# A planner's costs, homes and priorities changed in a two-layer hybrid decoder trunk

## The chip, the core and the metric

The kernel runs on one core of one Trainium2 chip. Times are device microseconds (us) of that core from the start to the end of one execution; the median of three is compared. A profile is one further execution taken by the hardware profiler. In it PE is TensorE (matrix products), PEld its loading of weights, DVE is VectorE, ACT is ScalarE, POOL is GpSimd and SP is the engine whose queue issues the DMA transfers. The text also uses the code's letters for them: V for DVE, A for ACT, G for POOL, Q for the DMA queue.

## The reference

16 meta tokens are put before 512 tokens of width 1024, and two layers run over the 528 rows, all in float32. Each layer is a half-step gated feed-forward network (FFN), a mixing block and a second FFN, with a norm before and after each:

```python
h = h + 0.5 * rms_norm(swiglu(rms_norm(h, g[0]), ffn_w_in[l, 0], ffn_w_out[l, 0]), g[1])
z = rms_norm(h, g[2]) @ w_in[l]            # 1024 -> 2476 columns
fq, fk, fv, ff, cu, lx, lg, dq, dkv, iq, ik, iw = jnp.split(z, split_at, axis=-1)
y_fox  = forgetting_attention(...)         # 4 heads x 64, keys q, k, v and a forget gate
y_conv = conformer_conv(cu, ...)           # gate, 31 taps per channel, layer norm, silu
y_lru  = rg_lru_branch(lx, lg, ...)        # 4 taps, a linear recurrence, times gelu(lg)
y_dsa  = dsa_attention(dq, dkv, iq, ik, iw, ...)   # 8 index heads choose 128 keys per query
mix = concatenate([y_fox, y_conv, y_lru, y_dsa]) @ w_out[l]
h = h + rms_norm(mix, g[3])
h = h + 0.5 * rms_norm(swiglu(rms_norm(h, g[4]), ffn_w_in[l, 1], ffn_w_out[l, 1]), g[5])
```

The index scores of a query are relu(q_idx . k_idx) summed over 8 heads with weights; the 128 best keys of each query are then attended to. The output is h without the meta rows.

## The kernel before

Activations lie with channels on the partitions and the 528 tokens along the free axis, in two halves of 264. Every weight is split on the chip into two fp32r parts, a copy by ACT (`wh`, `whi`) and the remainder by DVE or POOL (`wl`, `wlo`); a product x.W is three matmuls (hi.hi, hi.lo, lo.hi), 264 columns each. A weight tile of `w_in` or of the FFN is 1024 wide and split in two pieces of 512 in most places; an early tile of `w_out` is six rows of 128, split in two pieces of 384.

The mixing block of a layer (`mix`) goes through these steps. Four leading products (two for index queries, two for the recurrence), five token blocks (`token_block`: forget gate, latent, index key, index weight), then the column units (`column`) in the order of the string `ORDER`: c is the convolution's gate and value, v the attention's values, f its queries and keys, g the recurrence's gelu, q the queries of the sparse attention. Beside them run the index scores (`scores`: one matmul `psa<-KS,QS` per head and block, a relu by ACT into `rl`, and a multiply-add by DVE into `msel`), the choice of 128 keys (`choice`: 16 rounds of MAX8 and MATCH_REPLACE8 on DVE for each of four blocks), the 31 taps of the convolution (`conv_taps`: 8 taps per channel block on DVE as `cv<-hp,taps,cv`; the other 21 as a product by ACT into the one buffer `cm` and an add by POOL, `cv<-cv,cm`), the recurrence, and two attentions. Then comes the output projection: `early` adds up six of the eight row blocks, `late_rows` the last two, the sparse attention's; SP loads 15 early tiles and 2 late ones in each layer.

What runs when is not left to the hardware: a planner, `Weave`, builds the program. Every part above is a stream, a Python thread which stops before each instruction. `pick` takes the stream whose next instruction can start first by simulated clocks of PE, A, V, G and Q; among those that want the same engine and could start no more than `AHEAD` later, the one with the lowest `RANK` wins. `cost` gives the length of an instruction, `LATENCY` the time from one engine to another, `pace` multiplies PE's cost by 1.82 while TensorE's clock is taken to be halved, and `port` holds the intervals in which DVE and POOL exclude one another. The order that comes out is fixed on PE, A, V and G by dependencies between neighbours on an engine, so the chip executes each of these engines' work in just that order, and an instruction that is not ready holds up all behind it. All instructions of the planner are issued in `issue`, so that every one has line L252 in the profile; they are told apart by the names of their tiles.

Small elementwise operations have a home in the table `ENG`: V, G, or E for "whichever of the two ends first by the clocks". `wlead`, `wcol`, `wearly` and `wlate` are the weights' splits in the mixing block, `gelu` and `gate` scalings on either side of an activation function (tiles `xg` and `cv`), `rconv`, `rlru` and `rdsa` the splits of a branch's result into `ycat`. `SUMS` is the home of the adds of squares `acc`. PSUM has eight banks: two `u`, five `a`, one `n`; letter x in `LB` (leading FFN products) and `TB` (tails) takes `u` and `a` in turn.

## Time and profile before

| | us |
|---|---|
| median of 3 runs | 2126.69 (2126.13 to 2129.04) |
| profiled execution | 2126.25 |
| its span, first to last instruction | 2124.5 |
| PE busy in it | 2005.0 (94%) |
| DVE, ACT, POOL busy | 1252.5, 899.4, 475.3 |
| mean granted TensorE clock | 0.973 of full |

The span is 1.75 us shorter than the execution's time. In time order the span holds: the start (0 to 40 us), the first FFN of layer 0 (to 340), its mixing block (340 to 765), the second FFN (to 1055), a seam between the layers (to 1112), the first FFN of layer 1 (to 1425), its mixing block (to 1805), its second FFN (to 2095) and the end. In the page's picture of 40 slices PE shows a 9 through the FFNs and 7 or 8 in the mixing blocks, DVE 8 and 9 there and 3 or 4 elsewhere; the clock shows an 8 in the slices of the mixing blocks and a 9 in the rest.

### The profile page before, as it was taken

The numbers are of one execution on the slowest core, as the hardware profiler recorded it, in microseconds if no ns is written. First come the engines' busy times: TensorE is split into PE (matmuls) and PEld (weight loads), VectorE is DVE, ScalarE is ACT, GpSimd is POOL, SyncE is SP. The second block draws the span as 40 slices with busy tenths as digits, with TensorE's granted clock in tenths as the row PEclk, the third lists the DMA queues.
The fourth block names the chain that finished last, engine by engine and source line by source line (L and its number), as shares of the span: only waits on it lengthen the run. The fifth ranks groups of instructions, "written<-read, shape, count | busy, mean of one in ns | idle before, by whom it ended". The sixth has DMA issues, their size and how long they took to land.

```text
span 2124.5 us, 37005 instructions
## 1 busy us (share of the span) xinstructions
PE 2005.0 (94%) x14579; PEld 1880.8 (89%) x14579; DVE 1252.5 (59%) x2881; ACT 899.4 (42%) x1891; POOL 475.3 (22%) x429
## 2 busy tenths in 40 slices
PE   7999999978999899999989999999879998999998
PEld 7999999877878899999979999998768788888886
DVE  5434435889985843444384344447899958434444
ACT  5332233456765533222343322324568655332232
POOL 2101012336631110101221010123356412111121
PEclk9999999988999999999999999999889999999999
DMA  4432323211113233233223323322111132332321
GB/s 136 119 101 81 100 60 95 54 40 41 38 45 94 70 97 103 80 100 90 70 60 100 100 80 103 97 66 64 40 40 38 46 100 70 119 109 89 100 98 42
DMA packets 311078, 168.71 MB, mean 79 GB/s; under 512 B 15968, under 2 KB 302952, under 8 KB 310904
## 3 DMA queue, kind: packets, MB, share of 16 engines
q1 hardware_dynamic: 310616, 165.97, 26.9%
q8 instruction: 114, 1.87, 0.4%
q14 instruction: 60, 0.49, 0.1%
q10 hardware_dynamic: 288, 0.39, 0.1%
HBM read 164.22 MB, written 2.10 MB: 78 GB/s over the span
## 4 chain that ended last, share of the span: by engine, by line
PE 55%; DVE 21%; ACT 2%; issue 2%; SPq 1%; DMA 1%; POOL 0%; DVEq 0%; ACTq 0%; POOLq 0%
PE psa L252 39%; PE psu L252 15%; DVE msel L252 4%; DVE m L252 2%; DVE cv L252 2%; DVE hn L252 2%; PE psn L252 2%; DVE lra L252 2%; DVE acc L252 1%; DVE h L252 1%; DVE lrb L252 1%; SPq L252 1%; DVE x L252 1%; DMA wraw<-in_w_out_dram 1%; DVE rows L252 1%
## 5 line engine op out<-in xcount | busy, mean ns | idle before, releaser
L252 POOL TENSOR_TENSOR ga<-ga 128x264 f32<-128x264 f32 (+1 forms) x160 | 139.6, 874 | 1058.0 <-DVE ga L252 974.2
L252 ACT ACTIVATE whi<-wraw 128x512 fp32r<-128x512 f32 (+4 forms) x260 | 193.8, 757 | 248.7 <-PE psa L252 128.9
L252 PE MATMUL psa<-x,wh 128*128 128x264 f32 (+2 forms) x1228 | 244.8, 294 | 12.1 <-DVE x L252 4.7
L252 DVE TENSOR_TENSOR wlo<-wraw,whi 128x1024 fp32r<-128x1024 f32 (+4 forms) x179 | 179.4, 1008 | 122.1 <-ACT whi L252 120.1
L252 PE MATMUL psu<-x,whi 128*128 128x264 f32 (+1 forms) x1176 | 240.7, 300 | 6.1 <-DVE fq L252 2.7
L252 ACT ACTIVATE wh<-wraw 128x1024 fp32r<-128x1024 f32 (+3 forms) x188 | 151.3, 817 | 216.7 <-PE psa L252 117.1
L252 DVE TENSOR_TENSOR ga<-psa,R 128x264 f32<-128x264 f32 (+1 forms) x244 | 102.2, 428 | 233.5 <-PE psa L252 225.8
L252 DVE TENSOR_TENSOR wl<-wraw,wh 128x1024 fp32r<-128x1024 f32 (+3 forms) x161 | 161.4, 1011 | 127.4 <-ACT wh L252 126.3
L252 PE MATMUL psa<-x,whi 128*128 128x264 f32 (+2 forms) x1188 | 231.3, 291 | 1.0 <-DVE ga L252 1.0
L252 PEld LDWEIGHTS psa<-x,wh 128*128 128x128 f32 x1228 | 194.5, 189 | 20.4 <-DVE x L252 8.0
L252 PEld LDWEIGHTS psu<-x,whi 128*128 128x128 f32 x1176 | 192.8, 196 | 10.7 <-issue 4.2
L252 PEld LDWEIGHTS psa<-x,whi 128*128 128x128 f32 x1188 | 189.0, 191 | 2.9 <-DVE ga L252 1.1
L252 PE MATMUL psa<-x,wl 128*128 128x264 f32 (+2 forms) x614 | 178.4, 290 | 0.8 <-POOL wl L252 0.8
L252 PE MATMUL psa<-x,wlo 128*128 128x264 f32 (+2 forms) x594 | 173.1, 291 | 4.8 <-DVE wlo L252 4.8
L252 PE MATMUL psu<-x,wlo 128*128 128x264 f32 (+1 forms) x588 | 174.7, 298 | 0.0
L252 POOL TENSOR_TENSOR wlo<-wraw,whi 128x512 fp32r<-128x512 f32 (+1 forms) x81 | 116.2, 1440 | 235.9 <-ACT whi L252 207.1
L252 ACT ACTIVATE G<-ga 128x264 fp32r<-128x264 f32 (+1 forms) x160 | 67.5, 422 | 231.8 <-POOL ga L252 230.3
L252 PE MATMUL psa<-G,whi 128*128 128x264 f32 x852 | 156.4, 284 | 0.0
L252 PE MATMUL psa<-ycat,wh 128*128 128x264 f32 (+2 forms) x660 | 150.1, 318 | 3.8 <-DVE ycat L252 3.3
L252 POOL TENSOR_TENSOR cv<-cv,cm 128x528 f32<-128x528 f32 x84 | 126.4, 1505 | 91.7 <-ACT cm L252 91.6
L252 PEld LDWEIGHTS psa<-G,whi 128*128 128x128 f32 x852 | 131.8, 188 | 0.0
L252 DVE TENSOR_TENSOR G<-ga,G 128x264 fp32r<-128x264 f32 (+1 forms) x160 | 77.4, 484 | 90.3 <-ACT G L252 90.1
(306 smaller groups left out, 5030.9 us busy)
## 6 DMA issues: line engine op xcount, KB each, us to landing
wraw<-in_ffn_w_in_dram SPq DMA_DIRECT2D x160, 512.0 KB
wraw<-in_ffn_w_out_dram SPq DMA_DIRECT2D x44, 512.0 KB
wraw<-in_ffn_w_out_dram SPq DMA_DIRECT2D x48, 384.0 KB
wraw<-in_w_in_dram SPq DMA_DIRECT2D x36, 512.0 KB
wraw<-in_w_out_dram SPq DMA_DIRECT2D x180, 64.0 KB
xin<-in_x_dram SPq DMA_DIRECT2D x8, 256.0 KB
wraw<-in_w_out_dram SPq DMA_DIRECT2D x8, 256.0 KB
wraw<-in_w_in_dram SPq DMA_DIRECT2D x4, 256.0 KB
```

What stands on the lines that cost most here:

```text
L252: done = call(*args, **kw)
```

## The change

No product, sum or transfer is added or taken away: PE and ACT have as many instructions as before, and DVE and POOL together as well (DVE 2755 before, 2705 after; POOL 434 and 484). The numbers by which the planner reckons change, the homes of some operations, and with both the order on every engine. In the diff the tables of priorities are cut to a line of each side; all their other entries change as well in that manner (the rank of `prep` from 19.1 to 150.7, `scores` 52.9 to 13.7, `index` 212.2 to 217.3, `row` 179.1 to 100.5, `turn1` 25 to 168.8, `conv` 0 in both).

```diff
-    AHEAD = dict(PE=0.0, A=0.05, V=0.0, G=0.3)
+    AHEAD = dict(PE=0.0, A=0.19, V=0.0, G=0.3)
...
-            self.slow = part < (0.4 if self.slow else 0.25)
+            self.slow = part < 0.385
...
-    def ported(self, key, op, aps, reads):
...
+    def hold(self, key, op, aps, args, reads):
+        banks = any(a.space == bass.MemoryType.PSUM for a in aps)
+        if key == "G" or key == "V" and not banks and op not in ("max", "match_replace"):
+            return self.cost(key, op, aps, args, reads, 0.0)
+        return 0.0
...
         if key == "PE":
+            wide, rows = args[1].free_size(), args[1].shape[0]
+            load = 0.0127 + 0.00077 * wide
+            n = args[2].free_size()
+            stream = lambda t: max(t, load) if rows > 64 else t + load * (0.9 if rows != 32 else 0.3)
             if op == "transpose":
-                n = args[1].shape[0]
-                return self.pace(start, 0.091, n * n / 128 / 2400)
-            cols, rows = args[2].free_size(), args[2].shape[0]
-            if cols == 1:
-                return 0.156
+                return self.pace(start, stream(n / 1200 + 0.002), n * rows / 128 / 1200)
             if args[2].dtype == F32R:
-                return self.pace(start, max(cols / 2400 + 0.0115, 0.092), cols * rows / 128 / 2400)
-            return self.pace(start, max(cols * 4 / 2400 + 0.005, 0.184), cols * rows / 128 / 1200)
+                return self.pace(start, stream(n / 2400 + 0.0115), n * rows / 128 / 2400)
+            return self.pace(start, 2 * stream(n / 1200 + 0.002), n * rows / 128 / 600)
         if key == "V":
             one = op in ("tensor_scalar", "tensor_copy", "memset") and not psum
-            return (n / (2 if one else 1) + 66) / 960 + 0.06 * small
+            return (n / (2 if one else 1) + 66) / 960 + 0.06 * small + 0.06 * (op == "match_replace")
         if key == "A":
-            return n / 1200 + (0.05 if psum else 0.094) + 0.094 * small
+            extra = n > 8 and sum(a.free_size() == 1 for a in aps) > small
+            return n / 1200 + (0.05 if psum else 0.094) + 0.094 * small + 0.09 * extra
...
-    LB = 'a'
-    TB = 'ax'
+    LB = 'x'
+    TB = 'ux'
...
-    ORDER = 'ccvffgqqg'
+    ORDER = 'ccvffqgqg'
...
-    SUMS = dict(tail='G', late='V', enter='E')
+    SUMS = dict(tail='V', late='V', enter='E')
...
-    ENG = dict(hadd='V', wlead='G', wt='V', wcol='G', wearly='E', wlate='G', wtail='V', wnext='E', gelu='E',
-               geluo='V', gate='V', ct='V', tapsum='E', rfox='E', rconv='E', rlru='V', rdsa='E', lrua='V',
+    ENG = dict(hadd='V', wlead='E', wt='V', wcol='G', wearly='G', wlate='V', wtail='V', wnext='E', gelu='G',
+               geluo='V', gate='G', ct='V', tapsum='E', rfox='E', rconv='V', rlru='E', rdsa='G', lrua='V',
...
-    RANK = dict(ev=0, late=48.5, weights=18.0, row=179.1, lead=42.0, index=212.2, prep=19.1, scores=52.9,
+    RANK = dict(ev=6.3, late=48.5, weights=10.8, row=100.5, lead=49.3, index=217.3, prep=150.7, scores=13.7,
```

`free` and `start_of` take the duration of `hold` where they took a yes or no of `ported`, and follow the same rule with it; the constant 424 is written `QS0[-1]`, which is 424; the scratch tiles of one reciprocal root at the end of the kernel get one name instead of four.

Over the two layers the homes move as follows. The gate's scalings (8 TENSOR_SCALAR and 8 TENSOR_TENSOR on `cv`) and the gelu's (16 and 16 on `xg`) go from DVE to POOL. Of the 60 splits of 384 columns of `w_out`, POOL does 60 where it did 6; of the splits of 512 columns it does 82 where it did 102, DVE 94 where it did 74. DVE does 134 adds of squares `acc` where it did 98, POOL 6 where it did 42. Four splits of the attention's result go from POOL to DVE, and seven others come to POOL.

On PE, in the mixing block of layer 0, the index scores before stand in one run at their end. `KS,QS` is a score matmul, its last number the keys it covers; `x,wlo` and `x,whi` are column units.

```order
L252 MATMUL psu<-x,whi 128x264 x2
L252 MATMUL psu<-x,wlo 128x264
L252 MATMUL psa<-KS,QS 106x212 x3
L252 MATMUL psa<-KS,QS 104x264 x2
L252 MATMUL psa<-KS,QS 106x318 x4
L252 MATMUL psa<-KS,QS 106x424
L252 MATMUL psa<-KS,QS 104x264 x2
L252 MATMUL psa<-KS,QS 106x424
L252 MATMUL psa<-KS,QS 104x264 x2
L252 MATMUL psa<-KS,QS 106x424
L252 MATMUL psa<-KS,QS 104x264 x2
L252 MATMUL psu<-whi,x 106x256 x2
```

After, the same block's scores begin 89 matmuls sooner, counted from the start of the first FFN's tail (83 in layer 1), and stand one by one among column units:

```order
L252 MATMUL psa<-KS,QS 106x212
L252 MATMUL psu<-x,wlo 128x264
L252 MATMUL psu<-x,whi 128x264 x2
L252 MATMUL psa<-KS,QS 106x318
L252 MATMUL psu<-x,wlo 128x264
L252 MATMUL psu<-x,whi 128x264 x2
L252 MATMUL psu<-x,wlo 128x264
L252 MATMUL psa<-KS,QS 106x424
L252 MATMUL psu<-x,whi 128x264
L252 MATMUL psa<-KS,QS 106x212
L252 MATMUL psu<-x,whi 128x264
L252 MATMUL psu<-x,wlo 128x264
```

Columns that stood ahead of the first score stand between the scores now; the last 14 scores, `106x424` and `104x264`, still stand without a column between them.

On DVE the multiply-adds of the same scores (`msel<-rl,wh,msel`) alternate before with the DVE taps of the convolution:

```order
L252 SCALAR_TENSOR_TENSOR msel<-rl,wh,msel 106x212
L252 SCALAR_TENSOR_TENSOR cv<-hp,taps,cv 128x528
L252 SCALAR_TENSOR_TENSOR msel<-rl,wh,msel 106x212
L252 SCALAR_TENSOR_TENSOR cv<-hp,taps,cv 128x528
L252 SCALAR_TENSOR_TENSOR msel<-rl,wh,msel 106x212
L252 SCALAR_TENSOR_TENSOR cv<-hp,taps,cv 128x528
L252 SCALAR_TENSOR_TENSOR msel<-rl,wh,msel 106x212
L252 SCALAR_TENSOR_TENSOR cv<-hp,taps,cv 128x528
L252 SCALAR_TENSOR_TENSOR msel<-rl,wh,msel 106x318
L252 SCALAR_TENSOR_TENSOR cv<-hp,taps,cv 128x528
```

After, they stand nearly alone, and the convolution's input `hp` and its taps come behind them:

```order
L252 SCALAR_TENSOR_TENSOR msel<-rl,wh,msel 104x528
L252 TENSOR_SCALAR lrb<-lrb 128x264
L252 SCALAR_TENSOR_TENSOR msel<-rl,wh,msel 104x528
L252 TENSOR_TENSOR lrb<-lrb 128x264
L252 SCALAR_TENSOR_TENSOR msel<-rl,wh,msel 104x528
L252 TENSOR_TENSOR lrb<-lrb 128x264
L252 SCALAR_TENSOR_TENSOR msel<-rl,wh,msel 104x528
L252 TENSOR_TENSOR hp<-cv,psu 128x264
L252 MAX m_5336<-msel 106x8
L252 MAX m_5351<-msel 106x8
L252 TENSOR_TENSOR hp<-cv,psu 128x264
L252 MATCH_REPLACE msel<-m_5336,msel 106x212
```

The first `hp` of layer 0 stood four rows ahead of the first score's add before, and stands behind all but one of the scores' adds now; in layer 1 the first taps are moved behind most of them in the same way.

On POOL at the start of layer 0's taps (`cv<-cv,cm`) before there are only weight splits between the taps:

```order
L252 MEMSET hp 128x30
L252 MEMSET lf 128x640
L252 MEMSET hp 128x30
L252 TENSOR_TENSOR wlo<-wraw,whi 128x512 x3
L252 TENSOR_TENSOR cv<-cv,cm 128x528
L252 TENSOR_TENSOR wlo<-wraw,whi 128x512
L252 TENSOR_TENSOR cv<-cv,cm 128x528
L252 TENSOR_TENSOR wlo<-wraw,whi 128x512
L252 TENSOR_TENSOR cv<-cv,cm 128x528
L252 TENSOR_TENSOR wlo<-wraw,whi 128x512
L252 TENSOR_TENSOR cv<-cv,cm 128x528
```

After, the gate's scalings of `cv` come ahead of the first tap and between the first ones (8 in each layer); among the last taps and behind them, ahead of the first split of `w_out`, stand 14 operations on `xg`.

```order
L252 MEMSET lf 128x640
L252 MEMSET hp 128x30 x2
L252 TENSOR_SCALAR cv<-cv 128x264
L252 TENSOR_TENSOR cv<-cv,R 128x264
L252 TENSOR_TENSOR wlo<-wraw,whi 128x512
L252 TENSOR_SCALAR cv<-cv 128x264
L252 TENSOR_TENSOR cv<-cv,R 128x264
L252 TENSOR_TENSOR wlo<-wraw,whi 128x512 x3
L252 TENSOR_TENSOR cv<-cv,cm 128x528
L252 TENSOR_SCALAR cv<-cv 128x264
L252 TENSOR_TENSOR cv<-cv,R 128x264
L252 TENSOR_TENSOR cv<-cv,cm 128x528
```

At the seam of the layers on PE, the products that stand between a half's sum of squares (`ones,acc`) and the spreading of its result over the partitions (`cst,rows`) are 14 before:

```order
L252 MATMUL psn<-ones,acc 88x1 x3
L252 MATMUL psa<-x,wh 128x264
L252 MATMUL psa<-x,wl 128x264
L252 MATMUL psa<-x,wh 128x264 x2
L252 MATMUL psa<-x,wl 128x264
L252 MATMUL psa<-x,wh 128x264 x2
L252 MATMUL psa<-x,wl 128x264
L252 MATMUL psa<-x,wh 128x264 x2
L252 MATMUL psa<-x,wl 128x264
L252 MATMUL psa<-x,wh 128x264 x2
L252 MATMUL psa<-x,wl 128x264
L252 MATMUL psn<-cst,rows 128x88 x3
```

After, there are 37 matmuls between the same two, products of further weight tiles (`whi`, `wlo`) among them; the first of the 37:

```order
L252 MATMUL psn<-ones,acc 88x1 x3
L252 MATMUL psu<-x,wl 128x264
L252 MATMUL psa<-x,wh 128x264 x2
L252 MATMUL psa<-x,wl 128x264
L252 MATMUL psa<-x,wh 128x264 x2
```

23 matmuls more stand in this place, and 174 instead of 130 x.W products stand in all ahead of the fourth `ones,acc`.

## Rows read from the trace of the kernel before

**Rows 1.** Stretches: length; busy (count) of PE, PEld, DVE, ACT, POOL; clock, DMA, GB/s.
```profile
40.00:340.00 300.00, 300.00 (x2464) 299.81 (x2464) 127.05 (x218) 96.16 (x161) 30.02 (x40) 1.00 0.31 91
...
455.00:610.00 155.00, 134.25 (x949) 118.14 (x948) 151.38 (x417) 103.76 (x249) 91.28 (x65) 0.92 0.13 36
...
1055.00:1112.00 57.00, 46.17 (x354) 44.99 (x353) 46.60 (x122) 25.40 (x61) 17.43 (x14) 0.94 0.20 56
...
1525.00:1675.00 150.00, 132.84 (x951) 116.47 (x949) 148.05 (x413) 105.47 (x251) 94.60 (x64) 0.94 0.14 38
```

**Rows 2.** PE's waits, 455 to 610 us: total, times, longest.
```profile
PE psa L252 <- ACT rl L252: 11.5, 9, 4.5
```

**Rows 3.** PE's waits, 1525 to 1675 us.
```profile
PE psa L252 <- ACT rl L252: 10.1, 11, 2.3
```

**Rows 4.** PE's timeline, layer 0's run of scores: start, us, instruction, idle before.
```profile
471.88 0.70 PE L252 MATMUL psa<-KS,QS 128*106 128x212 f32 x5
477.11 0.60 PE L252 MATMUL psa<-KS,QS 128*106 128x318 f32 x1 [4.53 <-ACT rl L252]
...
490.77 0.63 PE L252 MATMUL psu<-whi,x 128*106 128x256 f32 x2
```

**Rows 5.** A stretch of ten microseconds inside that run.
```profile
480.00:490.00 10.00, 4.71 (x9) 2.35 (x10) 10.00 (x15) 5.06 (x13) 4.01 (x2) 0.50 0.20 52
```

**Rows 6.** DVE's groups by line, 455 to 610 us: busy, mean ns, idle before.
```profile
L252 DVE MATCH_REPLACE8 msel<-m,msel 106x212 f32<-106x212 f32 (+3 forms) x64 | 33.4, 525 | 0.0
L252 DVE MAX8 m<-msel 106x8 f32<-106x212 f32 (+3 forms) x64 | 32.4, 532 | 0.1
```

**Rows 7.** DVE's groups by form, whole span.
```profile
L252 DVE TENSOR_TENSOR wlo<-wraw,whi 128x384 fp32r<-128x384 f32 x26 | 15.3, 597 | 10.3 <-ACT whi L252 9.5 <-DMA wraw<-in_w_out_dram 0.5
...
L252 DVE TENSOR_TENSOR xg<-xg 128x264 f32<-128x264 f32 x16 | 9.3, 593 | 0.0
L252 DVE TENSOR_SCALAR xg<-xg 128x264 f32<-128x264 f32 x16 | 7.4, 474 | 0.0
L252 DVE TENSOR_TENSOR cv<-cv,R 128x264 f32<-128x264 f32 x8 | 6.4, 805 | 0.1
L252 DVE TENSOR_SCALAR cv<-cv 128x264 f32<-128x264 f32 x8 | 5.3, 668 | 2.0 <-ACT cv L252 2.0
```

**Rows 8.** POOL's groups by form, whole span.
```profile
L252 POOL TENSOR_TENSOR ga<-ga 128x264 f32<-128x264 f32 x120 | 93.7, 781 | 818.7 <-DVE ga L252 748.3 <-ACT ga L252 28.9 <-ACT whi L252 15.3
...
L252 POOL TENSOR_TENSOR wlo<-wraw,whi 128x384 fp32r<-128x384 f32 x6 | 6.9, 1152 | 59.8 <-ACT whi L252 59.8
L252 POOL TENSOR_TENSOR ycat<-fq,ycat 128x528 fp32r<-128x528 f32 x4 | 5.6, 1416 | 0.0
...
L252 POOL MEMSET small<- 128x512 f32 x2 | 1.1, 527 | 0.0
```

**Rows 9.** DVE's timeline at two places of layer 0's gate and taps.
```profile
452.46 1.40 DVE L252 TENSOR_TENSOR cv<-cv,R 128x264 f32<-128x264 f32 x1
...
473.34 0.42 DVE L252 TENSOR_TENSOR cv<-cv,R 128x264 f32<-128x264 f32 x1
```

**Rows 10.** POOL's timeline: two splits, first and last of layer 0's 42 taps.
```profile
450.97 2.60 POOL L252 TENSOR_TENSOR wlo<-wraw,whi 128x512 fp32r<-128x512 f32 x2 [12.12 <-ACT whi L252]
...
462.69 1.61 POOL L252 TENSOR_TENSOR cv<-cv,cm 128x528 f32<-128x528 f32 x1 [1.11 <-ACT cm L252]
...
605.96 1.32 POOL L252 TENSOR_TENSOR cv<-cv,cm 128x528 f32<-128x528 f32 x1 [0.85 <-ACT cm L252]
607.43 1.00 POOL L252 TENSOR_TENSOR wlo<-wraw,whi 128x384 fp32r<-128x384 f32 x1 [0.15 <-ACT whi L252]
```

**Rows 11.** The DMA queue's waits, 590 to 720 us.
```profile
SPq L252 <- POOL wlo L252: 38.6, 3, 24.5
```

**Rows 12.** PE's timeline at the seam of the layers.
```profile
1091.60 0.90 PE L252 MATMUL psn<-cst,rows 88*128 88x88 f32 x6 [3.15 <-DVE rows L252]
...
1103.39 0.45 PE L252 MATMUL psa<-x,wlo 128*128 128x264 f32 x1 [4.65 <-DVE wlo L252]
```

## What the changed kernel was predicted to take, and why

> **What bounds the kernel now.** I read the table of stretches first [rows 1]. From 40 to 340 us, the first FFN, PE is busy 300.00 of 300.00 us at clock 1.00 with 2464 matmuls: 300 / 2464 = 0.122 us for a product of 264 columns. A planner can gain nothing there, and the other FFNs read alike. What it can gain lies in the mixing blocks. From 455 to 610 PE idles 155 - 134.25 = 20.75 us, and runs at a mean clock of 0.92, which takes another 0.08 x 155 = 12.4 us of full speed. From 1525 to 1675 it is 17.2 idle and 0.06 x 150 = 9.0 and at the seam (1055 to 1112) 10.8 and 0.06 x 57 = 3.4. In the two middle stretches DVE is busy 151.38 of 155 and 148.05 of 150 us: there PE waits, and DVE sets the pace.
>
> The waits of PE say for what it stops: 11.5 us for `rl`, the relu of the index scores, in layer 0 [rows 2], 10.1 in layer 1 [rows 3]. The releaser named is ACT, but `rl` has three buffers, and DVE's adds free them. The timeline shows the place: from 471.88 to 490.77 PE has nothing but score matmuls in its order, and stops 4.53 us after the fifth [rows 4]. In ten microseconds of it DVE is busy 10.00, PE 4.71, and the granted clock is 0.50, the lower level of 1.2 GHz [rows 5]. POOL's 42 taps run from 462.69 to 605.96 + 1.32 = 607.28, and only then comes POOL's first split of `w_out` [rows 10]; behind that SP waits 38.6 us in three pieces [rows 11].
>
> **Scores among columns, taps behind scores (both layers).** In the new order two to four columns stand between most scores, and DVE no longer alternates score adds with taps. PE is thus filled where it stopped; but the columns are only moved: 89 matmuls stand behind the first score instead of ahead of it, 89 x 0.122 = 10.9 us in layer 0, 83 x 0.122 = 10.1 in layer 1. So no more than about 11 us a layer can be filled, and the 14 last scores still stand bare. The end of the stage is DVE's: its choice of keys, 33.4 + 32.4 us in layer 0 [rows 6], has to be done before the last attentions. So the gain is what DVE has less to do before that.
>
> DVE gives away, from the totals over two layers [rows 7]: gate 5.3 + 6.4, gelu 7.4 + 9.3, together 28.4, or 14.2 a layer. It takes over two result splits a layer; POOL needed 1.42 for one [rows 8], and I put DVE at half of that, 1.4 for both: net 12.8. POOL takes the work on. Its product of 264 columns takes 0.78 [rows 8]; its TENSOR_SCALAR is in no row, and I bound it by the MEMSET of 512 columns, 0.53, and the product, 0.78, and take the nearer in kind, the MEMSET. 12 of each: 12 x 0.78 + 12 x 0.53 = 15.7 us more on POOL a layer (18.7 by the other bound).
>
> POOL's work is not free for DVE. The same gate product took DVE 1.40 us at 452.46, while POOL worked on two splits until 453.57, and 0.42 at 473.34 with POOL idle [rows 9, 10]. The rule for it, in the Trainium skill's page "SBUF — State Buffer", section "SBUF: two separate sides", is that DVE and GpSimd share a port pair as an exclusive lock, held for a whole instruction, so that the later one blocks; 1.40 against 0.42 agrees with it. By that rule alone, with every POOL operation blocking DVE, the offload would be worth nothing; that is a rival below.
>
> MAX8 and MATCH_REPLACE8 show no such stretching: their means are 532 and 525 ns with 91.28 us of POOL beside them [rows 1, 6]. They and the readers of PSUM are more than half of DVE's time here, so I let less than half of POOL's 15.7 us come back as blocking, 7: net 12.8 - 7 = about 6 a layer. Ends: -14.2 (no blocking) and +2.9 (all of it blocking, 15.7 - 12.8).
>
> Against it stands the convolution. In layer 0 the first `hp` waited four rows ahead of the first score's add and now stands behind nearly all of them; even with the scores starting some 6 us sooner, the first taps come 10 to 20 us later. Before, 42 taps took 607.28 - 462.69 = 144.6 us, 3.44 each, where the last add takes 1.32 and waited 0.85 for its `cm` [rows 10], 2.2 in all, so that they can go closer together: at 2.6, my choice nearer to 2.2, they take 109, and 22 gate and gelu operations of 14.4 us come into the same queue ahead of the first split of `w_out`. 109 + 14 + 15 is about 138, near 144.6: I take half of the 6 back in layer 0, where the taps move furthest. Layer 0: -3. Layer 1, where DVE's order to the last choice is shortened most: -6. Ends of both: -14 and +12 each.
>
> **Splits of `w_out`.** 54 splits of 384 columns leave DVE, 27 a layer, and POOL needs 1.15 for 0.60 [rows 7, 8]. Two pieces a tile make a load's split 2.3 us instead of 1.2. That hides as long as loads arrive further apart; SP's waits of this stretch are for just these splits [rows 11]. If they stood bare it would be 27 x 0.55 = 15 a layer; hidden, zero. I take +1 a layer, near the hidden end, because the first tiles queue behind POOL's taps either way.
>
> **The seam.** PE stops 3.15 us for `rows` at 1091.60, and 4.65 for `wlo` at 1103.39 [rows 12]. With `LB` on seven banks, 23 more matmuls stand ahead of the first stop, 23 x 0.122 = 2.8 us, which nearly covers 3.15. In all 44 more products stand ahead of the fourth sum, 5.4 us, so up to 8.2 if both count. `wlo` is a weight split and comes as late as before: what PE does earlier is missing there. I take -4; ends -8 and +2 (the bare wait grown).
>
> **The rest.** The adds of squares moved to DVE lie beside PE-bound FFN tails, where DVE is busy 127 of 300 us [rows 1]: nothing; were that cover gone, 36 adds at the 0.59 of DVE's product of 264 columns [rows 7] would be 21 us over the whole kernel. The renamed scratch tiles and the constant: nothing.
>
> Sum: -3 - 6 + 2 - 4 = -11, from the profiled 2126.25 to 2115. That execution lies 0.44 us below the median of 2126.69, well inside what counts here.
>
> **Rivals.**
> 1. *POOL sets the end (slower).* The taps start 15 us later, and POOL's 22 added operations (14.4 us) are not taken in by closer taps, so that the convolution's last tap comes 10 us later in layer 0 and 6 in layer 1. The early output products need the convolution's result, so PE waits for it. For it: the first split after the taps began 0.15 us after them [rows 10], the queue is full at its end. Against: POOL idles 64 us of 155 in that stretch [rows 1]. It decides once the taps' mean stays above (144.6 - 15 - 14.4) / 42 = 2.74 us. Time: 2126.25 + 10 + 6 + 2 - 4 = 2140.
> 2. *Given back.* The scores fill PE and nothing ends sooner, since the output projection waits for its loads, which queue behind the taps (38.6 us [rows 11]). Only the seam is left: 2126.25 - 4 + 2 = 2124.
> 3. *All of POOL's work blocks DVE.* +2.9 in each layer instead of -12.8: 2126.25 + 6 - 4 + 2 = 2130. This is the Trainium skill's lock, taken at its full price. Against it stand the unstretched MAX8 rows.
> 4. *The clock stays up.* With columns among the scores PE is no longer granted 0.50 in them, and half of the idle and of the missing clock of both middle stretches comes back: (20.75 + 12.4) / 2 = 16.6 and (17.2 + 9.0) / 2 = 13.1, with the seam -4 and +2 for the splits: 2094. Against: DVE's choice of keys stays where it is.
>
> **How the numbers follow.** Forecast 0.42; rivals 1: 0.18, 2: 0.20, 3: 0.07, 4: 0.13. A measurement of this kernel can tell about 0.2%, 4.3 us, from no change. The forecast's own range is 2104 to 2124, so nearly all of its chance is on the faster side (0.38), rival 4 adds 0.13, and of rival 2, which lies 2.7 us below, a quarter falls beyond the bound (0.05): faster 0.56. Rival 1 is slower nearly always, rival 3 half the time, and a little of the forecast: 0.24. Within 0.2%: 0.20. The range leaves out half of rival 4 below and about half of rival 1 above: 2095 to 2138.
>
> **What would show it.** Right: PE's wait for `rl` falls from 11.5 and 10.1 to under 5 in sum, and the stretch of scores is no longer granted 0.50; `cv<-cv,R` is no DVE row any more; the last MATCH_REPLACE8 comes some 6 us sooner than the start of its layer's scores alone explains; at the seam the 3.15 is gone. Wrong: the last tap of layer 0 comes later against the start of its stage than 607.28 - 455 = 152 us and PE waits for `cv` behind it (rival 1); or PE is filled in the scores and idles as long before the output projection (rival 2).

## The result and the profile after

The changed kernel takes 2100.57 us (median; 2100.15 to 2101.61) against 2127.86 before (2126.13 to 2132.26): ratio 0.9869 (0.9852 to 0.9886). That is 26 to 27 us faster where 11 were forecast; the direction held, the size did not. Its span is 2098.4 us, 26.1 less. Ratios, here and below, are of fast runs alone; one run of four of `after_old_ranks`, 2212.66 us, was slow and is left out of its ratio.

The table of stretches of the kernel before, cut anew at events (first sum of the FFN's tail, first index score, last POOL tap, fourth sum at the block's end), for layer 0 and then layer 1:

```profile
core 0: us, PE busy (x) PEld busy (x) DVE busy (x) ACT busy (x) POOL busy (x), PEclk, DMA share, GB/s
360.40:455.90 95.50, 85.49 (x649) 79.91 (x650) 79.05 (x230) 48.18 (x112) 30.24 (x26) 0.91 0.20 50
455.90:607.30 151.40, 131.40 (x929) 115.81 (x928) 147.81 (x411) 101.15 (x244) 89.95 (x63) 0.92 0.13 35
607.30:738.20 130.90, 116.70 (x828) 105.91 (x827) 94.76 (x260) 77.06 (x199) 21.55 (x17) 0.95 0.28 82
1428.20:1525.90 97.70, 86.42 (x650) 80.77 (x649) 78.78 (x230) 48.49 (x112) 29.97 (x26) 0.91 0.18 46
1525.90:1672.60 146.70, 130.76 (x939) 115.00 (x940) 144.81 (x407) 102.30 (x244) 92.78 (x62) 0.94 0.14 38
1672.60:1795.90 123.30, 109.06 (x808) 100.58 (x807) 94.56 (x261) 76.09 (x197) 25.13 (x21) 0.97 0.29 85
```

The same stretches of the changed kernel:

```profile
358.60:446.00 87.40, 73.27 (x564) 68.35 (x564) 74.02 (x234) 46.08 (x108) 11.46 (x12) 0.85 0.20 51
446.00:597.20 151.20, 139.54 (x993) 126.65 (x994) 143.40 (x402) 102.97 (x245) 100.97 (x81) 0.93 0.14 38
597.20:723.70 126.50, 114.51 (x850) 108.08 (x849) 81.86 (x224) 78.12 (x198) 50.65 (x53) 0.96 0.29 85
1405.20:1490.90 85.70, 71.90 (x567) 67.17 (x565) 73.86 (x234) 46.10 (x108) 11.48 (x12) 0.86 0.20 52
1490.90:1643.00 152.10, 135.19 (x996) 121.83 (x997) 148.71 (x409) 103.31 (x248) 98.53 (x80) 0.97 0.13 37
1643.00:1770.60 127.60, 111.42 (x828) 105.03 (x827) 82.28 (x218) 76.88 (x196) 53.05 (x53) 0.96 0.28 82
```

Call the three A, B and C. A is 8.1 us shorter in layer 0 and 12.0 in layer 1, with 85 and 83 fewer matmuls. B takes up 64 and 57 more and changes by -0.2 and +5.4; C by -4.4 and +4.3. The blocks give 12.7 and 2.3 us. The rest lies between them: up to the first tail's sum -1.8, second FFN of layer 0 -3.7 (319.2 to 315.5 us, where before its first 21.8 us were granted 0.84 and did 157 matmuls, now 1.00 and 182), seam with the next FFN -4.8 (370.8 to 366.0), the end -0.8. Together 26.1. A stretch of one profile scatters by some us: in `before_lead_banks` below, with the blocks' order unchanged, layer 0's C is 127.6 instead of 130.9 and its block 375.6 instead of 377.8.

PE's side of it: a block holds as many matmuls as before (2406 and 2407 records in layer 0, 2397 and 2391 in layer 1). Its busy time falls by 6.3 and 7.7 us; its idle time falls by 6.4 in layer 0 and grows by 5.4 in layer 1.

What PE waits for, in B of layer 0, of layer 1, and at the seam (1039 to 1093 us); these answer to [rows 2], [rows 3] and [rows 12]:

```profile
PE psu L252 <- DVE gt L252: 4.7, 1, 4.7
PE psa L252 <- ACT rl L252: 2.2, 4, 1.2
...
PE psu L252 <- DVE gt L252: 6.3, 2, 5.8
...
PE psa L252 <- ACT rl L252: 0.8, 1, 0.8
...
PE psn L252 <- DVE acc L252: 2.8, 1, 2.8
PE psn L252 <- DVE rows L252: 1.6, 1, 1.6
```

The wait for `rl` is all but gone, 11.5 and 10.1 down to 2.2 and 0.8; the wait for `gt`, the evacuation of a column, has grown from 1.2 and 1.4 to 4.7 and 6.3. At the seam the 4.7 for `wlo` is gone and the longest wait for `rows` is 1.6 where it was 3.2, but 2.8 for `acc` has come. POOL's taps of layer 0, first and last, and what follows [rows 10]:

```profile
475.72 1.32 POOL L252 TENSOR_TENSOR cv<-cv,cm 128x528 f32<-128x528 f32 x1
...
595.85 1.32 POOL L252 TENSOR_TENSOR cv<-cv,cm 128x528 f32<-128x528 f32 x1 [0.89 <-ACT cm L252]
599.89 0.41 POOL L252 TENSOR_SCALAR xg<-xg 128x264 f32<-128x264 f32 x1 [2.71 <-ACT xg L252]
...
607.37 1.00 POOL L252 TENSOR_TENSOR wlo<-wraw,whi 128x384 fp32r<-128x384 f32 x1
```

They start 13 us later and end 10 us sooner: 121.5 us for 42, 2.89 each, with half of the gate's and of the gelu's operations in between. Against the first score the last tap ends as before (B, 151.2 and 151.4 us), and the first split of `w_out` starts at the same time of the span, 607.37 and 607.43.

The last round of DVE's choice of keys, in layer 0 before and after, then in layer 1 before and after:

```profile
606.22 0.69 DVE L252 MATCH_REPLACE8 msel<-m,msel 104x528 f32<-104x528 f32 x1
...
582.15 0.70 DVE L252 MATCH_REPLACE8 msel<-m,msel 104x528 f32<-104x528 f32 x1
...
1694.35 0.69 DVE L252 MATCH_REPLACE8 msel<-m,msel 104x528 f32<-104x528 f32 x1
...
1631.39 0.69 DVE L252 MATCH_REPLACE8 msel<-m,msel 104x528 f32<-104x528 f32 x1
```

The choice ends 14.2 us sooner after the first score in layer 0 (151.0 to 136.8) and 28.0 sooner in layer 1 (169.1 to 141.2). From its end to the block's fourth sum it is 140.9 us where it was 131.3, and 138.5 where it was 100.9.

The forms that are new on POOL, over the whole span [rows 7, 8]:

```profile
L252 POOL TENSOR_TENSOR wl<-wraw,wh 128x384 fp32r<-128x384 f32 x32 | 32.7, 1040 | 46.2 <-ACT wh L252 33.3 <-DMA wraw<-in_w_out_dram 12.4 <-PE psa L252 0.4
...
L252 POOL TENSOR_TENSOR xg<-xg 128x264 f32<-128x264 f32 x16 | 13.8, 861 | 0.8
L252 POOL TENSOR_SCALAR xg<-xg 128x264 f32<-128x264 f32 x16 | 9.2, 572 | 14.4 <-DVE rows L252 8.1 <-ACT xg L252 5.8
...
L252 POOL TENSOR_TENSOR cv<-cv,R 128x264 f32<-128x264 f32 x8 | 7.4, 930 | 0.7
L252 POOL TENSOR_SCALAR cv<-cv 128x264 f32<-128x264 f32 x8 | 4.9, 614 | 51.3 <-ACT cv L252 51.3
```

### The profile page after: what moved, and what is told of

It is laid out like the page before. It is cut to its first block, busy times and chain, and to the rows that moved or that the text cites. A ratio compares the mean times of both kernels' runs of the same rounds, so it can differ in the third digit from the quotient of the medians.

```text
span 2098.4 us, 36992 instructions
## 1 busy us (share of the span) xinstructions
PE 1989.9 (95%) x14579; PEld 1880.4 (90%) x14579; DVE 1223.5 (58%) x2831; ACT 900.0 (43%) x1891; POOL 487.6 (23%) x479
## 5 line engine op out<-in xcount | busy, mean ns | idle before, releaser
L252 PE MATMUL psu<-x,whi 128*128 128x264 f32 (+1 forms) x1108 | 231.3, 302 | 15.8 <-DVE gt L252 10.9
L252 DVE TENSOR_TENSOR wlo<-wraw,whi 128x1024 fp32r<-128x1024 f32 (+3 forms) x166 | 171.3, 1040 | 127.3 <-ACT whi L252 126.5
L252 PE MATMUL psa<-x,wh 128*128 128x264 f32 (+2 forms) x1148 | 225.9, 294 | 2.7 <-ACT x L252 2.1
L252 DVE TENSOR_TENSOR wl<-wraw,wh 128x1024 fp32r<-128x1024 f32 (+2 forms) x140 | 153.0, 1098 | 117.4 <-ACT wh L252 116.7
L252 PEld LDWEIGHTS psa<-x,wh 128*128 128x128 f32 x1148 | 182.5, 191 | 6.7 <-ACT x L252 3.0
L252 PE MATMUL psu<-x,wlo 128*128 128x264 f32 (+1 forms) x554 | 165.3, 299 | 3.2 <-POOL wlo L252 3.2
L252 PE MATMUL psa<-x,wl 128*128 128x264 f32 (+2 forms) x574 | 167.2, 291 | 0.0
L252 PE MATMUL psa<-ycat,wh 128*128 128x264 f32 (+2 forms) x612 | 135.6, 314 | 3.9 <-ACT ycat L252 2.7
L252 PE MATMUL psa<-ycat,whi 128*128 128x264 f32 (+2 forms) x552 | 121.6, 314 | 0.0
L252 PEld LDWEIGHTS psa<-x,wlo 128*128 128x128 f32 x628 | 118.7, 189 | 0.9
```

The costliest lines, as they stand in the source:

```text
L252: done = call(*args, **kw)
```

## The experiments

Each is compared with the kernel before or the changed kernel ("after"); a ratio is to the kernel before. The first theories: START (DVE paces B from the first score on, so what PE does ahead of the first score is on the path) and OFFLOAD (the gain is DVE's lighter load).

**The lead splits and the offload.** `before_wlead` and `after_wlead_pool` change one word each; the other two issue the gate and gelu on the other engine but let the planner reckon as if not, so that the order stays.

```diff
 before_wlead       wlead='G' -> wlead='E'      (in the kernel before)
 after_wlead_pool   wlead='E' -> wlead='G'      (in the changed kernel)
 after_held_gates   gate, gelu: planned for POOL, issued on DVE
 before_held_gates  gate, gelu: planned for DVE, issued on POOL
+class Held:
+    def __getattr__(self, op):
+        call = getattr(self.real, op)
+        return lambda *args, **kw: self.weave.issue(self.key, op, call, args, kw, self.home)
...
+        key = home or key          # in issue(), ahead of the dependency that fixes the order
```

> The kernel before with one word changed: the splits of the mixing block's four leading weight tiles (wlead) go to whichever of DVE and POOL ends first, instead of to POOL. The planner then puts the first index score 79 matmuls sooner in layer 0 (3339 instead of 3418 ahead of it) and the convolution's taps behind half of the score adds. Theory START (the stretch from the first score to the last choice of keys is paced by DVE, so that what PE does ahead of the first score is on the path, and columns moved behind it are absorbed there): 79 x 0.122 = 9.6 us a layer at most, 10 to 18 us faster than before, with the first score 7 to 12 us sooner in each layer and the stretch from there to the convolution's sums no longer than 152 and 148 us. Theory OFFLOAD (the gain is DVE's lighter load, gate and gelu on POOL): nothing is offloaded here, so within 4 us of before.

> The changed kernel with wlead back on POOL, all else of the change kept; the planner puts the first score 158 matmuls later than in the changed kernel (3490 instead of 3332). Theory START: slower than the changed kernel by 10 to 18 us (2110 to 2119), the first scores 8 us or more later. Theory OFFLOAD: gate and gelu stay on POOL, so within 4 us of the changed kernel's 2100.6.

> The changed kernel with its order held, but the gate's and the gelu's scalings (48 operations over both layers) issued on DVE in the places where the planner put them on POOL. DVE gets back 28.4 us by the rows of before, POOL loses 35. Theory OFFLOAD: slower than the changed kernel by 8 to 20 us. Theory START: the pace of DVE's stretch grows by what of it falls ahead of the last choice of keys, at most the gates (5.9 us a layer): slower by 3 to 10 us, of which the larger part in layer 0.

> The kernel before with its order held, but the gate's and the gelu's scalings issued on POOL in the places where they stood on DVE. Theory OFFLOAD: faster than before by 8 to 20 us. Theory START: the first scores come no sooner, the gain is DVE's share alone, less what POOL's port blocks: 0 to 8 us faster.

Measured: 2140.26 (1.0056, 1.0039 to 1.0073), 2152.77 (1.0116, 1.0101 to 1.0131), 2105.85 (0.9900, 0.9885 to 0.9915), 2131.00 (1.0016, 1.0007 to 1.0025). The offload is worth 5.3 us in the new order and costs 3.3 in the old one, where neither theory expected a loss; OFFLOAD as the cause falls. START falls too as it stood: `before_wlead` has A shorter by 4.1 and 6.4 us, but B longer by 5.7 and 16.3. But without the lead splits on DVE the changed kernel loses 52 us, where START expected 10 to 18: A is 111.8 and 111.6, worse than before.

**Seam, taps, buffers, costs.**

```diff
 before_lead_banks         LB = 'a' -> 'x'
 before_taps_behind_scores wait(f"conv{b}") -> wait(f"conv{b}", "scores")
 after_two_cm              TEMPS: cm=1, t1=5 -> cm=2, t1=4
 after_old_costs           class Weave of the kernel before in the changed kernel
```

> The kernel before with LB = 'x' alone: the leading products of the next FFN use seven PSUM banks instead of five; the order in the mixing blocks stays that of before. Theory SEAM (the bank count alone lets 44 products be done in the seam's idle time): the stretches from the first ones,acc of the seam to the next tail (50.1 + 320.7 us by the fourth sum) fall together by 4 to 6 us, the whole by 4 to 6 us (2122). Rival: wlo is a split and comes as late as before, so the products only move the stop: within 2 us of before.

> The kernel before, with one more event waited for by the convolution's taps: none starts ahead of the last index score. Theory TAPS (ACT's product for a tap stands in ACT's order among the scores' relus, which wait for DVE's adds, and DVE's taps stand among those adds, so that both chains hold each other up): the taps start some 30 us later in layer 0 but take 2.8 to 3.0 us each instead of 3.44 (118 to 126 instead of 144.6 us), the scores' run is shorter by 5 us or more, and the whole is within 8 us of before. Rival QUEUE (POOL's own work sets the taps' pace): they take 3.3 us or more each, the conv sums come 20 us later or more and the whole is 15 us slower or more.

> The changed kernel with two buffers cm instead of one for the taps' products (and four t1 instead of five, for the room). ACT's next product need not wait for POOL's add then. Theory TAPS: the pair ACT-POOL with one buffer sets the pace of the taps (2.89 us each in layer 0); with two it comes down to 2.3 to 2.6 (POOL's add and the splits between), the last tap comes 8 us or more sooner, and the whole gains 0 to 6 us, as far as DVE's choice of keys allows. Theory START (DVE's stretch ends the stage): last tap sooner, the whole within 3 us.

> The changed kernel's tables (homes, priorities, banks, ORDER) under the planner of before (its costs, pace, AHEAD). The first score keeps its early place (3332 matmuls ahead of it), but columns stand between nearly all scores and 18 DVE taps stand among the scores' adds again. Theory START with TAPS: the stretch from the tail to the first score stays at 86 to 88 us, that from there to the last tap grows by 5 us or more in each layer: 2108 to 2125. Rival (the planner's costs move only the last digits): within 4 us of 2100.6.

Measured: 2126.90 (0.9991, 0.9978 to 1.0004), 2129.99 (1.0009, 0.9992 to 1.0026), 2206.35 (1.0359, 1.0337 to 1.0381), 2169.34 (1.0184, 1.0162 to 1.0206). The banks alone give nothing. Taps behind the scores cost nothing to speak of, but take 137 and 122 us, between the two theories. With two `cm` the taps take 86 us, 2.05 each, as theory TAPS wanted or better; and yet the whole is 106 us slower than the changed kernel, PE stopping once for 22.7 us in layer 0 behind a split of POOL. So earlier taps by themselves bring no earlier end; the order changed with the buffers, and where the 106 us come from is not shown. The old costs lose 69 us, where 8 to 25 were expected, with A as short as after (87.8, 88.4): the loss lies behind the first score. B of layer 0 in three pieces and C, with the old costs:

```profile
444.60:504.60 60.00, 52.59 (x398) 51.32 (x398) 57.77 (x149) 32.23 (x67) 34.83 (x31) 0.93 0.14 37
504.60:544.60 40.00, 30.08 (x205) 27.04 (x203) 37.54 (x80) 26.77 (x57) 27.98 (x21) 0.93 0.25 68
544.60:595.70 51.10, 40.09 (x212) 28.90 (x211) 44.59 (x133) 33.72 (x85) 30.77 (x22) 0.76 0.05 15
595.70:760.30 164.60, 148.72 (x1045) 135.66 (x1044) 93.01 (x267) 91.26 (x238) 57.34 (x60) 0.94 0.23 65
```

and in the changed kernel:

```profile
446.00:506.00 60.00, 51.80 (x346) 48.83 (x347) 58.24 (x144) 30.73 (x70) 31.77 (x24) 0.85 0.13 36
506.00:546.00 40.00, 36.76 (x280) 34.54 (x279) 38.72 (x121) 30.69 (x71) 29.20 (x24) 0.96 0.20 54
546.00:597.20 51.20, 50.99 (x371) 43.28 (x370) 46.44 (x139) 41.55 (x105) 40.00 (x34) 1.00 0.10 27
597.20:723.70 126.50, 114.51 (x850) 108.08 (x849) 81.86 (x224) 78.12 (x198) 50.65 (x53) 0.96 0.29 85
```

In the last 51 us of B PE does 371 matmuls at full clock in the one, 212 at a mean clock of 0.76 in the other. The matmuls of columns and values alone (tile `psu`) in the third piece, first with the old costs, then in the changed kernel:

```profile
544.60:595.70 51.10, 1.49 (x4) 0.76 0.05 15
```
```profile
546.00:597.20 51.20, 25.26 (x176) 1.00 0.10 27
```

With the old costs the columns are eaten up ahead of the attentions: 365, 174, 4 in the three pieces, against 302, 180, 176 after. Hence a third theory, FILLER: columns, which wait for next to nothing, must last to the end of the attentions, since PE else idles and runs at the lower of its two clocks for part of it.

The kernel before is not short of columns there. Its last piece of B, all of PE's work, and then the tile `psu` alone in the first and the last piece:

```profile
555.90:607.30 51.40, 50.33 (x356) 42.38 (x356) 50.34 (x161) 38.93 (x102) 33.04 (x23) 1.00 0.06 16
...
455.90:515.90 60.00, 36.39 (x266) 0.86 0.11 31
...
555.90:607.30 51.40, 29.03 (x191) 1.00 0.06 16
```

So FILLER can say what the old costs lose with the new homes, and not what the changed kernel gains on the kernel before.

**FILLER.**

```diff
 before_no_column_ahead      in column(i):  + wait("scored")     # fired by the first score's matmul
 after_old_costs_rationed    in column(i):  + if i >= 4: wait("scores")
 before_tail_sums_on_dve     SUMS tail='G' -> 'V'
 after_old_ranks             RANK of the kernel before in the changed kernel
```

> The kernel before with one rule more: no column unit starts ahead of the layer's first score matmul. The first score then has 3322 matmuls ahead of it instead of 3418, and 272 column matmuls still stand among the attentions (277 before). Theory START with FILLER (the stretch from the first score on is paced by DVE; columns put behind the first score are absorbed there, so long as some are left for the attentions): tail to first score 8 to 12 us shorter in each layer, first score to last tap no more than 4 us longer, the whole 10 to 20 us faster (2108 to 2118). Theory HOMES (only with gate, gelu and wlead moved does the early score pay): within 5 us of before or slower.

> The changed kernel's tables under the planner of before, as in after_old_costs (2169), with one rule more: column units from the fifth on wait for the last score. 286 columns then stand among the attentions, as in the changed kernel (277), where after_old_costs had 144. Theory FILLER (what the new costs bring is that columns last to the end of the attentions, so that PE neither idles nor is granted 1.2 GHz there): the attentions' stretches recover, 2105 to 2130. Rival DETAIL (the new costs set many small orders right, the columns are not what matters): above 2150.

> The kernel before with SUMS tail = 'V' alone: the adds of squares in the FFN tails on DVE. The order in the mixing blocks is that of before; at the seam 37 matmuls stand behind the third sum instead of 14, and 316 instead of 275 ahead of the fourth, the same as in the changed kernel. Theory SEAM2 (those products, and not LB, are the seam's gain): seam and next FFN together fall from 370.8 to 365 to 367 us, the whole by 3 to 6 us. Rival: within 2 us of before.

> The changed kernel with the priorities of before. First score as early as in the changed kernel (3322 matmuls ahead), no DVE tap among the score adds; 163 columns stand among the attentions in layer 0 and 288 in layer 1 (277 in the changed kernel). Theory FILLER: layer 0 loses 8 to 25 us in its attentions, layer 1 under 8: 2108 to 2135. Rival DETAIL (priorities matter by many small orders): both layers lose about alike.

Measured: 2137.73 (1.0052, 1.0034 to 1.0070), 2133.15 (1.0021, 1.0009 to 1.0033), 2156.36 (1.0135, 1.0104 to 1.0165), 2107.06 (0.9901, 0.9883 to 0.9919). Rationing the columns by hand gives back 36 of the 69 us, a little less than the range expected: with 169 of them in B's last piece PE does this there:

```profile
544.00:588.70 44.70, 44.29 (x336) 38.63 (x335) 39.42 (x112) 33.99 (x86) 32.42 (x29) 1.00 0.12 31
```

C stays at 147.1 (126.5 after): FILLER is about half of what the costs bring. Holding the columns back in the kernel before does not help: A shrinks by 2.1 and 5.4 us only, though 96 matmuls have gone from it. What PE waits for in layer 0's A then, and A's row:

```profile
PE psa L252 <- DVE rs0k L252: 7.6, 1, 7.6
PE psa L252 <- DVE wh L252: 4.4, 1, 4.4
```
```profile
361.60:455.00 93.40, 71.38 (x553) 65.33 (x553) 75.09 (x223) 46.45 (x108) 27.75 (x24) 0.86 0.19 48
```

So A has a second limit, DVE's chain to the index keys (`rs0k` is their norm). POOL is busy 27.75 us beside it, 11.46 in the changed kernel, where the lead splits went elsewhere. The old priorities cost about 6 us, none of it in the mixing blocks: A, B and C together are 1.5 and 3.6 us shorter than after, layer 0 with its 163 columns too, against FILLER's forecast; the FFNs and the seam are longer (321.2 against 315.5 and 370.7 against 366.0 us). The tail's sums alone cost 28 us, though the score's order stayed; C grew by 8.3 and 17.3 us, which no run here explains.

**Homes and costs, each and both.**

```diff
 before_new_homes        ENG and SUMS of the changed kernel in the kernel before
 before_new_costs        class Weave of the changed kernel in the kernel before
 before_homes_and_costs  both
 after_wearly_either     wearly='G' -> 'E' in the changed kernel
```

> The kernel before with the changed kernel's homes (ENG and SUMS), its own planner and priorities. First score early (3334 matmuls ahead), 492 column matmuls among the scores and 192 among the attentions, in one lump before their middle. Theory FILLER: tail to first score 86 to 92 us, the attentions starve: 2130 to 2165. Rival HOMES (DVE's lighter load pays by itself): faster than before, 2105 to 2122.

> The kernel before with the changed kernel's planner (costs, pace, AHEAD), its own homes and priorities. 96 columns still stand ahead of the first score, 224 columns among the attentions in layer 0 and 275 in layer 1. Theory FILLER: first stretch as before (95 to 98 us), the rest within 10 us a layer: 2122 to 2145. Rival COSTS (truer costs pay by themselves): faster than before, 2105 to 2120.

> The kernel before with the changed kernel's homes and planner, its own priorities, ORDER and banks. The planner orders the two layers differently: layer 0 with 3490 matmuls ahead of the first score and 144 columns among the attentions (384 among the scores), layer 1 with the score as early as in the changed kernel and 276 among the attentions. Theory FILLER: layer 0's mixing block takes 380 us or more from the tail's first sum to its fourth (before 377.8, changed 365.1), layer 1's 360 to 368 (before 367.7, changed 365.4). Rival PAIR (homes and costs together pay wherever): both layers alike, within 5 us of each other.

> The changed kernel with the early splits of w_out (wearly) on whichever of DVE and POOL ends first. Layer 0's order up to the attentions is that of the changed kernel; layer 1's becomes the same as layer 0's: no DVE tap among the score adds and 88 columns among the scores instead of 280, as many among the attentions. Theory FILLER: layer 1's first score to fourth sum falls from 279.7 to 273 to 278 us; the splits go faster as well, up to 5 us a layer: 2090 to 2100. Rival: w_out's splits on DVE press its tail sums: within 3 us or slower.

Measured:

| | old costs | new costs |
|---|---|---|
| old homes | 2126.7 to 2128.7 (before) | 2127.63, 0.9996 (0.9982 to 1.0010) |
| new homes | 2186.38, 1.0268 (1.0235 to 1.0300) | 2119.16, 0.9955 (0.9941 to 0.9969) |

The new costs alone do nothing in sum, the new homes alone lose 58 us, both gain 9. But the nothing is made of two parts. A, B and C of layer 0 with the new costs alone:

```profile
361.50:456.50 95.00, 84.53 (x654) 78.91 (x654) 79.92 (x229) 47.97 (x111) 30.08 (x26) 0.95 0.20 51
456.50:599.90 143.40, 127.24 (x909) 110.58 (x909) 142.28 (x403) 102.02 (x244) 94.82 (x65) 0.93 0.14 37
599.90:724.40 124.50, 114.62 (x848) 105.00 (x846) 94.93 (x266) 77.77 (x197) 25.19 (x17) 0.99 0.30 86
```

Layer 0's block takes 362.9 us, 14.9 less than before and 2.2 less than in the changed kernel, with the first score no sooner; layer 1's takes 381.1, 13.4 more. Why the two go apart no run here explains; the expectation had each within 10 us.

With the homes alone A is as short as after (88.1, 87.8), the columns run out again (350, 145, 16), and C is 169.2 and 165.9 us. In `before_homes_and_costs` the planner ordered the layers differently:

```profile
361.10:465.10 104.00, 92.94 (x723) 88.01 (x723) 85.64 (x246) 52.80 (x119) 25.09 (x25) 0.90 0.21 53
465.10:604.60 139.50, 120.05 (x839) 103.42 (x840) 134.57 (x373) 97.70 (x240) 92.66 (x69) 0.94 0.12 33
604.60:734.40 129.80, 117.15 (x846) 108.26 (x844) 92.17 (x242) 77.88 (x193) 59.52 (x54) 0.95 0.29 83
1419.60:1504.60 85.00, 71.19 (x556) 66.60 (x554) 74.00 (x231) 46.10 (x108) 11.78 (x12) 0.86 0.21 53
1504.60:1660.90 156.30, 144.50 (x1007) 130.37 (x1008) 146.03 (x407) 104.56 (x249) 97.49 (x80) 0.92 0.14 36
1660.90:1787.10 126.20, 110.50 (x809) 103.53 (x808) 83.32 (x222) 76.40 (x194) 52.00 (x52) 0.95 0.29 83
```

Layer 0, late score and few columns left: 373.3 us; layer 1, early score, columns rationed: 367.5. Layer 0 is better than the 380 that FILLER expected, and 5.8 apart is hardly more than the 5 of the rival: this run decides between them neither way. `after_old_ranks` differs from this kernel only in ORDER, TB and LB (and the renamings) and takes 12 us less, 9.7 in layer 0's block and 5.7 in layer 1's. LB does nothing, in the kernel before and, below, in the changed one; ORDER and TB were not changed by themselves, so that nearly half of the gain hangs on a part that no run splits. `after_wearly_either`, 2111.80 (0.9916, 0.9888 to 0.9944), is 11 us slower than the changed kernel; B and C grew in both layers (280.4 and 283.2 against 277.7 and 279.7), layer 1's against FILLER's forecast. The time is as the rival had it; as the order changed with the engine, that the splits themselves are better off on POOL is not shown.

**The seam again.**

```diff
 after_lead_banks_back   LB = 'x' -> 'a' in the changed kernel
 before_new_ranks        RANK of the changed kernel in the kernel before
```

> The changed kernel with LB = 'a' again: the order of every engine stays, the leading products have five PSUM banks instead of seven. Theory BANKS (the seam's gain needs the banks, together with the order): seam and next FFN together rise from 366.0 to 369 to 372 us, the whole by 3 to 6 us. Theory RANKS (the priorities bring the next FFN's weight splits earlier, so that PE no longer waits 4.7 us for wlo): 366 us as in the changed kernel, the whole within 3 us.

> The kernel before with the changed kernel's priorities alone; LB and the tail sums as before, 35 matmuls behind the third sum of the seam (14 before, 37 changed). Theory RANKS: seam and next FFN fall from 370.8 to 365 to 368 us and the wait for wlo is gone. Theory BANKS: 369 us or more. The mixing blocks are placed badly by theory FILLER (192 columns ahead of the first score, 144 among layer 0's attentions): the whole is slower than before, 2135 to 2165.

Measured: 2101.52 (0.9873, 0.9852 to 0.9895) and 2152.14 (1.0115, 1.0094 to 1.0135). Seam and FFN take 366.2 us with five banks: LB does nothing. With the priorities alone they take 372.1, with the tail's sums alone 369.3, without the priorities 370.7, before 370.8, after 366.0. So neither does it alone; that it takes both was not tried.

## Why the prediction was wrong

**The failed step** is "The end of the stage is DVE's ... So the gain is what DVE has less to do before that." DVE's choice of keys came 14.2 and 28.0 us sooner after the first score, where 6 were forecast, and 22.3 and 40.0 us sooner after the tail's first sum; the blocks became 12.7 and 2.3 us shorter. So its end does not set the end of the block, least of all in layer 1. In the last piece of layer 0's B it is PE that is full: 50.99 of 51.20 us at clock 1.00.

By terms, the splits of `w_out` taken into the layers: layer 0 was put at -2 and came to -12.7, layer 1 at -5 and came to -2.3, the seam at -4 and came to -4.8, the rest at nothing and came to -6.3. So the shortfall is layer 0's term, of which half had been taken back for the convolution, and the rest, of which 3.7 us lie in layer 0's second FFN. That the sum had the right sign is in part luck: layer 1, its largest term, gave less than half of what was forecast, and most of the gain came where little or nothing had been.

**What the runs show in its place** is where the time went, and not one cause. A is 8.1 and 12.0 us shorter, near the cap of 10.9 and 10.1 that the forecast had worked out and put aside because the columns "are only moved". In layer 0 it was wrong to put it aside: B took them in for nothing (929 to 993 matmuls, 151.4 to 151.2 us), out of the 20 us of idle time that the first paragraph had counted. In layer 1 it was nearly right: B and C gave back 9.7 of the 12.0. A short A is not enough, as `before_wlead`, `before_new_homes` and `after_old_costs` show, and a gain of this size in layer 0 does not need it, as `before_new_costs` shows. Why layer 0 gains and layer 1 does not stays open.

**What made A shorter** is not the planner's place for the columns alone, as `before_no_column_ahead` shows, but the homes too, `wlead` among them, a word that the forecast did not weigh. Undone, it cost 52 us, the most of the words that were undone one by one.

**What the costs are for.** The homes bring the early score and, under the old planner, empty the columns too soon; the new costs keep some for the attentions, as the kernel before did. Shown: the third piece with and without, in four kernels, and 36 us back by rationing alone. The other half of the costs' 69 us stays open.

**The offload** was set at 6 us a layer; held order shows 5.3 for both layers, and -3.3 in the old order. That its port term was too small is likely and not shown by itself: POOL's products took 0.86 to 0.93 us in the mean instead of 0.78, and the TENSOR_SCALAR 0.57 to 0.61 instead of 0.53. The rival by which all of it blocks DVE was worth 6 us slower; the old order lost half of that. The lock of the Trainium skill ("SBUF — State Buffer", "SBUF: two separate sides"), by which the later of the two engines waits, agrees with these in kind. How much of the wait is whose, no run separates.

**The convolution** was feared to come late: 109 us for the taps, 14 for the gate and gelu and 15 for the late start made 138 from the old first tap to the first split of `w_out`. Measured are 121.5 for the taps with half of that work between them, and 144.7 to the split, as before; the last tap came 10 us sooner. The rival of POOL's queue, whose sign was a later last tap, did not come in, though at 2.89 us a tap the mean lay above the 2.74 that the forecast gave as its point: the early score gave the slack. In `after_two_cm` the taps were 35 us shorter still and the end was not sooner.

**The seam** was -4 and came to -4.8, by luck, for the reason given is wrong: seven banks do nothing.

**The splits of `w_out`** on POOL take 1.03 to 1.04 us, were put at +1 a layer; in the one run that let the planner choose their engine, and with it the order, the kernel was 11 us slower, so they may be a gain.

**The clock rival** (2094) is nearest in time but not by its reason: layer 0's first 60 us of B, with the scores, are granted 0.85 in the mean where they were granted 0.86, and the last 51 us had full speed before as well. B's mean clock rose from 0.92 to 0.93 in layer 0 and from 0.94 to 0.97 in layer 1.

## What to carry to other kernels

Where an engine paces a stretch, ask when the stretch begins, and then what ends the one behind it: work moved from ahead of its first instruction to behind it is a gain only as far as idle time takes it in, all of it in layer 0 here and little in layer 1. Work that waits for nothing is a stock: an order that spends it early pays at the end, in idle time and in clock. And parts of a planner's change can't be priced one by one: here homes alone cost 58 us, costs alone nothing in sum (14.9 gained in one layer, 13.4 lost in the other), both gained 9, with ORDER, TB and LB 21, and with the priorities 27.

## What the runs showed of the hardware

TENSOR_SCALAR of 264 float32 columns on POOL, which no row of before showed, takes 0.41 us at its shortest and 0.57 to 0.61 in the mean here. With a second `cm` the pair of ACT and POOL does a tap in 2.05 us instead of 2.89 to 3.44, POOL's own add being 1.3 to 1.4.
